# RMSNorm with ReLU on one core: the last store's last row divided between SyncE and GpSimd

## Chip, core and metric

One NeuronCore of a Trainium2 chip. The metric is the device time of one execution in microseconds (us), median of several. One profiled execution of each kernel gives the trace; its span, from the first to the last instruction, is about 1.8 us shorter than the device time of the same execution.

## The reference

```python
# x: 16 x 1024 x 512 float32, gamma: 512 ones, eps: 1e-5
rms = np.sqrt(np.mean(x ** 2, axis=-1, keepdims=True) + eps)
return np.maximum(x / rms * gamma, 0).astype(np.float32)
```

33.6 MB are read and 33.6 MB written; each row of 512 numbers is normalized by itself.

## The kernel before

The 16384 rows lie as 8 chunks of 128 partitions by K = 16 rows, so one partition's part of a chunk is 32 KB in one piece, in memory and in its slot. There are 6 slots. SyncE issues all large DMAs and waits in between; GpSimd only passes on semaphores; ScalarE makes sums of squares and square roots; VectorE the rest.

```python
    def store(i):
        nc.sync.dma_start(out=ov[i], in_=slot_ap(i)).then_inc(sem_slot[i % nslots], 16)

    with tc.tile_critical():
        # ... the first six chunks' loads
        for i in range(nchunks):
            nc.sync.wait_ge(done, per * (i + 1))
            store(i)
            # ... wait for a free slot and load the next chunk
        for m, (i, a, r) in enumerate(loads):
            loaded(nc.gpsimd, m)
            nc.gpsimd.sem_inc(ready, r // G)
        # ... ScalarE and VectorE loops; each half chunk ends with then_inc(done, 1)

    with nc.sync.register("landed") as landed:          # all stores have landed
        nc.sync.reg_mov(landed, 32)
        for s in range(nchunks - nslots, nslots):
            nc.sync.wait_ge(sem_slot[s], landed)
        nc.sync.reg_mov(landed, 64)
        for s in range(nchunks - nslots):
            nc.sync.wait_ge(sem_slot[s], landed)
```

At the end of the block `tile_critical` the framework has SyncE, ScalarE, VectorE and GpSimd each execute a DRAIN instruction (all four stand on that line in the traces), and SyncE waits for the others before it goes on to the waits named `landed`.

Of the kernel before, what the change touches and what calls it, by code (L numbers as in the profile page):

```python
# [12 lines left out]
@with_exitstack  # L13
def kernel(
    ctx: ExitStack,
    tc: tile.TileContext,
    x: bass.AP,
    gamma: bass.AP,
    eps: bass.AP,
    out: bass.AP,  # L20
):



    nc = tc.nc
    P = nc.NUM_PARTITIONS

    x2 = x.flatten_outer_dims()
    out2 = out.flatten_outer_dims()
    n, d = x2.shape  # L30
    rows = n // P
    inv_d = 1.0 / d
    K = 16
    G = 8
    nchunks = rows // K
    nslots = 6
    ngroups = rows // G
    per = K // G
    xv = x2.rearrange("(c p k) d -> c p k d", p=P, k=K)
    ov = out2.rearrange("(c p k) d -> c p k d", p=P, k=K)  # L40

    singles = ctx.enter_context(tc.tile_pool(name="singles", bufs=1))
    psum = ctx.enter_context(
        tc.tile_pool(name="psum", bufs=1, space=bass.MemoryType.PSUM))

    gseed = singles.tile([P, d], F32, name="gseed")
    gamma_sb = singles.tile([P, d], F32, name="gamma_sb")
    eps_sb = singles.tile([P, 1], F32, name="eps_sb")
    ss = singles.tile([P, rows], F32, name="ss")
    rms = singles.tile([P, rows], F32, name="rms")  # L50
    rstd = singles.tile([P, rows], F32, name="rstd")
    slots = singles.tile([P, nslots * K * d], F32, name="slots")
    junk = psum.tile([P, G, d], F32, name="junk")


    loads = [(0, 0, G), (0, G, K - G)] + [(i, 0, K) for i in range(1, nchunks)]


    sem_half = tc.alloc_semaphore("half")
    sem_slot = [tc.alloc_semaphore(f"slot{s}") for s in range(nslots)]  # L60
    sem_g = tc.alloc_semaphore("gam")
    sem_z = tc.alloc_semaphore("zero")
    ready = tc.alloc_semaphore("ready")
    sq = tc.alloc_semaphore("sq")
    done = tc.alloc_semaphore("done")
    sa = tc.alloc_semaphore("sa")
    sv = tc.alloc_semaphore("sv")

    def slot_ap(i):
        s = (i % nslots) * K * d  # L70
        return slots[:, s:s + K * d].rearrange("p (k d) -> p k d", d=d)

    def load(m):
        i, a, r = loads[m]
        nc.sync.dma_start(out=slot_ap(i)[:, a:a + r, :],
                          in_=xv[i][:, a:a + r, :]
                          ).then_inc(sem_half if m == 0 else sem_slot[i % nslots], 16)

    def loaded(engine, m):
        i = loads[m][0]  # L80
        if m == 0:
            engine.wait_ge(sem_half, 16)
        else:
            engine.wait_ge(sem_slot[i % nslots], 32 * (i // nslots) + 16)

    def store(i):
        nc.sync.dma_start(out=ov[i], in_=slot_ap(i)).then_inc(sem_slot[i % nslots], 16)

    ctx.enter_context(tc.manual_schedule(engines={mybir.EngineType.SP}))
    with tc.tile_critical():  # L90
        for m, (i, a, r) in enumerate(loads):
            if i < nslots:
                load(m)
        nxt = nslots
# [3 lines that stand above are left out]
            if i >= 1 and nxt < nchunks:  # L98
                nc.sync.wait_ge(sem_slot[nxt % nslots], 32)
                for m, (c, a, r) in enumerate(loads):  # L100
                    if c == nxt:
                        load(m)
                nxt += 1

        for m, (i, a, r) in enumerate(loads):
            loaded(nc.gpsimd, m)
            nc.gpsimd.sem_inc(ready, r // G)

        nc.vector.memset(gseed, 0.0).then_inc(sem_z, 1)  # L109
        nc.vector.memset(eps_sb, eps).then_inc(sem_z, 1)  # L110

        nc.scalar.wait_ge(sem_z, 1)
        nc.scalar.dma_start(out=gseed[0:P:32, :],
                            in_=gamma[None, :].to_broadcast([P // 32, d])
                            ).then_inc(sem_g, 16)
        nc.scalar.preload_act_table(ACTF.Sqrt)  # L116
        nc.scalar.wait_ge(sem_z, 2)
        with nc.scalar.Fori(0, ngroups) as gi:
            nc.scalar.wait_ge(ready, 1)
            nc.scalar.sem_inc(ready, -1)  # L120
            base = nc.scalar.snap((gi % (nslots * per)) * (G * d))
            col = nc.scalar.snap(gi * G)
            for j in range(G):
                a = nc.scalar.activation(  # L124
                    out=junk[:, j, :], in_=slots[:, bass.ds(base + j * d, d)],
                    func=ACTF.Square, accum_out=ss[:, bass.ds(col + j, 1)])
                if j == G - 1:
                    a.then_inc(sa, 1)
            nc.scalar.wait_ge(sa, 1)
            nc.scalar.sem_inc(sa, -1)  # L130
            nc.scalar.activation(out=rms[:, bass.ds(col, G)], in_=ss[:, bass.ds(col, G)],  # L131
                                 func=ACTF.Sqrt, bias=eps_sb, scale=inv_d).then_inc(sq, 1)

        nc.vector.wait_ge(sem_g, 16)
        nc.vector.stream_shuffle(gamma_sb, gseed, [0] * 32)  # L135
        with nc.vector.Fori(0, ngroups) as gi:
            nc.vector.wait_ge(sq, 1)
            nc.vector.sem_inc(sq, -1)  # L138
            base = nc.vector.snap((gi % (nslots * per)) * (G * d))
            col = nc.vector.snap(gi * G)  # L140
            blk = slots[:, bass.ds(base, G * d)]
            nc.vector.reciprocal(out=rstd[:, bass.ds(col, G)],  # L142
                                 in_=rms[:, bass.ds(col, G)]).then_inc(sv, 1)
            nc.vector.wait_ge(sv, 1)
            nc.vector.sem_inc(sv, -1)  # L145
            for j in range(G):
                row = slots[:, bass.ds(base + j * d, d)]
                r = nc.vector.scalar_tensor_tensor(  # L148
                    out=row, in0=row, scalar=rstd[:, bass.ds(col + j, 1)], in1=gamma_sb,
                    op0=ALU.mult, op1=ALU.mult)  # L150
                if j == G - 1:
                    r.then_inc(sv, 1)
            nc.vector.wait_ge(sv, 1)
            nc.vector.sem_inc(sv, -1)  # L154
            nc.vector.tensor_scalar_max(out=blk, in0=blk, scalar1=0.0).then_inc(done, 1)  # L155

    with nc.sync.register("landed") as landed:
        nc.sync.reg_mov(landed, 32)
        for s in range(nchunks - nslots, nslots):
            nc.sync.wait_ge(sem_slot[s], landed)  # L160
        nc.sync.reg_mov(landed, 64)
        for s in range(nchunks - nslots):
            nc.sync.wait_ge(sem_slot[s], landed)


# [33 lines left out]
```

## Time and profile before

| | before |
|---|---|
| device time, median of 6 | 162.75 us (162.68 to 163.0) |
| span | 160.9 us |
| DMA engines busy with SyncE's queue | 97.6% |
| last store issued | 146.46 us |
| last closing packet, its landing | 159.39 us, 159.88 us |
| SyncE's branch after its last wait | 159.95 us |

A store ends on each DMA engine with a packet of 4 B, the closing packet, and its increment of the semaphore lands some tenths of a us later (0.36 us for most engines and 0.49 for the last in this trace). The views that carry this stand in the prediction below and are not repeated. Of a line's instructions a view gives name, count, ns least/median/most, first and last start in us; on the line that ends the block (L90), SyncE's NOP is where it goes on when all others have drained.

```profile
L90 SPq NOP  x2: 13/13/13, 0.7 to 147.2; - x2
L90 POOLq DRAIN  x1: 41/41/41, 146.9 to 146.9; - x1
```

GpSimd's drain takes 41 ns, and at 147.2 us, 12.7 us before the last landing, SyncE is past the block. It then goes through its waits for the older slots while the last store is still running. When this lands, only the end of that wait and the branch are left before the closing barrier.

### The profile page before, as it was taken

Reading aid. Unit: us, or ns where it says so; the run is one execution under the profiler, and the core shown is the slowest. Engines: PE = TensorE matmul, PEld = TensorE weight load, DVE = VectorE, ACT = ScalarE, POOL = GpSimd, SP = SyncE. Lnnn points to the kernel's source line nnn. Section 1 sums busy time; section 2 is a strip of 40 time slices with the busy share of each in tenths; the row PEclk is TensorE's granted clock in tenths of the full one; section 3 lists DMA queues with packets and bytes.
Section 4 is the critical chain, followed back from the end, with each engine's and each line's share of the span. In section 5 each row is a group of like instructions: output and inputs, shape, how many; then the busy total and the mean of one; then the engine's idle time right before and its main releaser. Section 6 shows DMA issues by size and latency. Waiting matters only on the chain. (4 is left out here: it accounts for less than half of the span.)

```text
span 160.9 us, 1006 instructions
## 1 busy us (share of the span) xinstructions
DVE 126.0 (78%) x164; ACT 86.3 (54%) x273; POOL 0.2 (0%) x4
## 2 busy tenths in 40 slices
DVE  1103989898989899999999999999999999994000
ACT  3088929889988988988900198503994000000000
POOL 0000000000000000000000000000000000000000
DMA  5999999999999998999999999999999999999993
GB/s 155 434 432 415 521 391 391 513 399 391 489 424 391 481 432 367 415 391 489 424 391 489 424 391 448 464 391 440 456 407 432 456 415 424 464 415 424 464 407 138
DMA packets 2456, 67.12 MB, mean 417 GB/s; under 512 B 276, under 2 KB 276, under 8 KB 280
## 3 DMA queue, kind: packets, MB, share of 16 engines
q1 hardware_dynamic: 2448, 67.11, 97.6%
q10 hardware_dynamic: 8, 0.01, 0.0%
HBM read 33.56 MB, written 33.55 MB: 417 GB/s over the span
## 5 line engine op out<-in xcount | busy, mean ns | idle before, releaser
L124 ACT ACTIVATE junk<-slots 128x512 f32 x128 | 74.5, 582 | 30.6 <-ACTq L120 30.3
L148 DVE SCALAR_TENSOR_TENSOR slots<-slots,rstd,gamma_sb 128x512 f32 x128 | 86.2, 747 | 4.8 <-DVEq L145 4.8
L155 DVE TENSOR_SCALAR slots<-slots x16 | 36.7, 2294 | 2.4 <-DVEq L154 0.2
L124 ACT ACTIVATION_READ_ACCUMULATOR junk<-slots x128 | 23.9, 187 | 0.0
L142 DVE RECIPROCAL rstd<-rms x16 | 3.1, 196 | 6.3 <-DVEq L138 6.3
L131 ACT ACTIVATE rms<-ss,eps_sb x16 | 4.8, 301 | 3.0 <-ACTq L130 3.0
L135 DVE LOAD_MASK_SELECT gamma_sb<-gseed x1 | 0.0, 14 | 5.8 <-DMA gseed<-in_gamma_dram 5.8
L116 ACT ACT_TABLE_LOAD x1 | 1.3, 1283 | 2.8 <-issue 2.8
L109 DVE MEMSET gseed<- 128x512 f32 x1 | 0.5, 485 | 1.1 <-SPq L90 1.1
L135 DVE STREAM_SHUFFLE gamma_sb<-gseed 128x512 f32<-128x512 f32 x1 | 0.7, 715 | 0.0
L180 POOL MEMSET const-bfloat16-1.0<- 128x1 bf16 x1 | 0.1, 103 | 0.0
L180 POOL MEMSET const-uint8-127<- 128x1 uint8 x1 | 0.1, 102 | 0.0
L180 POOL MEMSET const-float32-0.0<- 128x1 f32 x1 | 0.1, 100 | 0.2 <-issue 0.2
L180 POOL MEMSET const-float32-1.0<- 128x1 f32 x1 | 0.1, 99 | 0.0
L110 DVE MEMSET eps_sb<- 128x1 f32 x1 | 0.1, 59 | 0.0
## 6 DMA issues: line engine op xcount, KB each, us to landing
out_dram<-slots SPq DMA_DIRECT2D x8, 4096.0 KB, 31.3
slots<-in_x_dram SPq DMA_DIRECT2D x7, 4096.0 KB, 30.3
slots<-in_x_dram SPq DMA_DIRECT2D x2, 2048.0 KB, 9.6
gseed<-in_gamma_dram ACTq DMA_DIRECT2D x1, 8.0 KB
```

The source lines that it names most:

```text
L109: nc.vector.memset(gseed, 0.0).then_inc(sem_z, 1)
L110: nc.vector.memset(eps_sb, eps).then_inc(sem_z, 1)
L116: nc.scalar.preload_act_table(ACTF.Sqrt)
L124: a = nc.scalar.activation(out=junk[:, j, :], in_=slots[:, bass.ds(base + j * d, d)], func=ACTF.Square, accum_out=ss[:, bass.ds(col + j, 1)])
L131: nc.scalar.activation(out=rms[:, bass.ds(col, G)], in_=ss[:, bass.ds(col, G)], func=ACTF.Sqrt, bias=eps_sb, scale=inv_d).then_inc(sq, 1)
L135: nc.vector.stream_shuffle(gamma_sb, gseed, [0] * 32)
L142: nc.vector.reciprocal(out=rstd[:, bass.ds(col, G)], in_=rms[:, bass.ds(col, G)]).then_inc(sv, 1)
L148: r = nc.vector.scalar_tensor_tensor(out=row, in0=row, scalar=rstd[:, bass.ds(col + j, 1)], in1=gamma_sb, op0=ALU.mult, op1=ALU.mult)
L155: nc.vector.tensor_scalar_max(out=blk, in0=blk, scalar1=0.0).then_inc(done, 1)
L180: nc = _bacc.Bacc("TRN2", target_bir_lowering=False, num_devices=1)
```

## The change

The packet records of the trace show one DMA engine ending the last store alone, 0.37 us after the next. The change is to give the engine thought to be it (the fifth, number 4) less to do: the last row of the last store goes to other engines, by way of GpSimd's DMAs.

```diff
+    parts = [(0, P, 0, K)]
+    tail = [(0, P, 0, K - 1), (125, P, K - 1, K)]
+    tail_pool = [(0, 5, K - 1, K), (5, 125, K - 1, K)]
+
+    def store_part(engine, i, part, sem):
+        p0, p1, k0, k1 = part
+        engine.dma_start(out=ov[i][p0:p1, k0:k1, :], in_=slot_ap(i)[p0:p1, k0:k1, :]
+                         ).then_inc(sem, 16)
+
     def store(i):
-        nc.sync.dma_start(out=ov[i], in_=slot_ap(i)).then_inc(sem_slot[i % nslots], 16)
+        for part in (tail if i == nchunks - 1 else parts):
+            store_part(nc.sync, i, part, sem_slot[i % nslots])
@@ in the block, after GpSimd's loop
+        nc.gpsimd.wait_ge(done, ngroups)
+        for part in tail_pool:
+            store_part(nc.gpsimd, nchunks - 1, part, sem_tail)
@@ at the end
-        nc.sync.reg_mov(landed, 64)
+        nc.sync.wait_ge(sem_tail, landed)
         for s in range(nchunks - nslots):
+            last = tail if s == nchunks - nslots - 1 else parts
+            nc.sync.reg_mov(landed, 48 + 16 * len(last))
             nc.sync.wait_ge(sem_slot[s], landed)
```

## The prediction

> **What bounds the kernel now.** I read the page first, then the SyncE queue's waits, then the DMA view in ever narrower windows around the end. The page of the kernel before:
>
> ```profile
> span 160.9 us, 1006 instructions
> DVE 126.0 (78%) x164; ACT 86.3 (54%) x273; POOL 0.2 (0%) x4
> DMA  5999999999999998999999999999999999999993
> DMA packets 2456, 67.12 MB, mean 417 GB/s; under 512 B 276, under 2 KB 276, under 8 KB 280
> q1 hardware_dynamic: 2448, 67.11, 97.6%
> ```
>
> The DMA engines are full in 38 of 40 slices, while the busiest compute engine, DVE, has 22% idle. All of it is one queue, q1, that SyncE issues: nine loads and eight stores. So the kernel is bound by 67.1 MB through 16 DMA engines, and compute ends early: the last DVE instruction runs from 144.14 for 2.29 us (timeline), and the last store is issued at 146.46. What SyncE's own queue waits for from there on, and the line where it waits:
>
> ```profile
> SPq L87 <- DVE slots L155: 16.1, 1, 16.1
> SPq L163 <- DMA out_dram<-slots: 12.4, 1, 12.4
> ...
> DMA to landing us min/median/max: 13.4/31.3/41.0
> ```
>
> The last 12.4 us are a wait for a store. The least time to landing, 13.4 us, is the last store's: 146.46 + 13.4 = 159.9 us. The span ends 1.0 us later, after the closing barrier. A store of 4096 KB is 128 packets of 32 KB, 8 for each of 16 engines, and one packet of 4 B for each engine that announces its end. The DMA view from 149.72 to 158.3, inside the last store:
>
> ```profile
> DMA packets 112, 3.67 MB, mean 428 GB/s; under 512 B 0, under 2 KB 0, under 8 KB 0
> q1 hardware_dynamic: 112, 3.67, 99.0%
> ```
>
> 0.990 x 16 x 8.58 us / 112 = 1.213 us for 32 KB. The view from 5.7 to 6.4 us, where the small gamma load runs on q10, gives the price of a 2 KB packet:
>
> ```profile
> q10 hardware_dynamic: 4, 0.01, 3.0%
> ```
>
> 0.030 x 16 x 0.7 / 4 = 0.084 us. A straight line through both is 0.009 us a packet plus 0.0376 us a KB; it gives 0.611 us for 16 KB, which is what the packet records of the first two half loads show. So a 30 KB packet should take 1.138 us.
>
> Which engine ends last? The closing 4 B packets in 158.3 to 158.9, in 158.95 to 159.1, and in 159.1 to 159.45:
>
> ```profile
> DMA packets 13, 0.00 MB, mean 0 GB/s; under 512 B 13, under 2 KB 13, under 8 KB 13
> ...
> DMA packets 2, 0.00 MB, mean 0 GB/s; under 512 B 2, under 2 KB 2, under 8 KB 2
> ...
> DMA packets 1, 0.00 MB, mean 0 GB/s; under 512 B 1, under 2 KB 1, under 8 KB 1
> ```
>
> 13 of 16 engines are done by 158.9 (the records say 158.37 to 158.82), two at 159.01 and 159.03, and a single one at 159.40. Their announcements land about 0.36 us after the packet for the others, and 0.49 us for the last (159.37 and 159.88). The records of the earlier stores show one engine falling behind: the last closing packet trails the next by 0.02 us near 110.6, then by 0.09 near 120.4, 0.19 near 130.2, 0.29 near 140.0, 0.37 near 149.7 and 0.37 at 159.4. So the end of the kernel is one DMA engine's lag, some 0.4 to 0.5 us. That is what this change aims at.
>
> [...] The trace before has no GpSimd DMA and no engine numbers: it neither confirms the numbering nor says that the late engine is number 4. [...]
>
> **The change part by part.** Bytes are the same. Removed: the last store's row 15 from all packets, so SyncE's main piece has 128 packets of 30 KB, 8 an engine: 8 x 1.138 = 9.10 us instead of 8 x 1.213 = 9.70. Moved: row 15 as 128 packets of 2 KB: 5 and 120 by GpSimd, 3 (partitions 125 to 127) by SyncE[...]. Per engine, if the dealing is as intended:
> - number 4: 9.10 + 1 x 0.084 = 9.19 us, 0.52 less than now;
> [...]
>
> If the late engine is number 4, it ends at 159.40 - 0.52 = 158.88 and lands at about 159.37. The next two, at 159.01 and 159.03 now, become last[...]; plus 0.36 to land, 159.46 to 159.63. Against 159.88 this saves 0.42 to 0.25 us, 0.35 in the middle. Costs: GpSimd's two issues[...] begin at 146.46 and lie beside 12 us of transfers; SyncE's second issue (0.33 us, as its issues show) as well; extra closing packets, 0.01 us each. The wait on the tail's semaphore comes before those on slots 0 and 1, and two more register moves: under 0.1 us, and only if GpSimd's part lands last. [...] I put these costs at 0.07 us in all. Sum: -0.35 + 0.07 = about -0.28 us, so 162.72 - 0.28 = 162.44.
>
> **The rivals.**
> First, the skipped engine is not the late one[...]. Then the late engine gets 0.07 to 0.24 us more, and the time is 162.8 to 163.0. Against it: an edit this particular was surely made by someone who knew the late engine; for it: nothing in the trace says which engine it is. I give it 25%.
> Second, a new wait takes the place: [...] its small packets[...] drain after the main piece. With 12 us of room I expect little, [...] 163 us or more: 10%.
> Third, using GpSimd for DMA at all adds something at start or end ([...] a longer drain in the closing barrier). Nothing in the profile speaks for it: GpSimd's drains take 34 to 88 ns now. If it did, 163 to 165 us: 5%.
> Fourth, the lag is random from execution to execution. Against it: three runs within 0.32 us, and the same engine falling behind over several stores. Then the gain would fade to about 0.1.
>
> **Range and chances.** The largest possible gain is perfect balance: the mean engine ends near 158.7, so 0.7 us, 0.4%. A 2% change is 3.25 us and would need a fixed cost that nothing shows. Intended course 162.25 to 162.55; rivals up to about 163; so 162.44, range 162.15 to 163.0, and 1%, 98%, 1%.
>
> **What would show it.** Right: a new GpSimd queue with 125 packets of 2 KB and its closing packets, 128 packets of 30 KB at 1.138 us in q1, closing packets of the main piece within 158.4 to 159.3 and none at 159.4, the last landing near 159.5 instead of 159.88, the span near 160.6. Wrong: one engine still alone at 159.4 or later (first rival); GpSimd's 2 KB packets after the 30 KB ones (second); the distance from the last landing to the end of the span over 1.0 us, or the unprofiled time further than 1.8 us from the span (third).

The sum is -0.35 + 0.07 = -0.28 us, so 162.44. The saving of 0.42 to 0.25 us was made with assumed shares: one 2 KB piece for number 4, as stands above, and 8 to 10 for each of the other engines, which was to make the next two 0.07 to 0.24 us later (159.10 to 159.27). The 0.07 us of costs held 0 to 0.1 us for the small packets' turns. The cut guess at the length of GpSimd's issues is not in the sum; in the result's trace they took 0.63 and 0.55 us. The shares were never shown; what the traces show instead is told under the experiments.

## The result

The changed kernel took 163.5 us (163.3 to 163.74, 6 runs) against 162.75 (162.68 to 163.0, 6 runs). The ratio is 1.0044, interval 1.0031 to 1.0057. So it is 0.75 us slower by the medians, within 2%, but outside the predicted range, and on the other side of the time before than the 162.44 predicted.

The page of the changed kernel:

```profile
span 161.8 us, 1009 instructions
DVE 126.0 (78%) x164; ACT 86.3 (53%) x273; POOL 1.4 (1%) x6
...
DMA packets 2575, 67.12 MB, mean 415 GB/s; under 512 B 327, under 2 KB 327, under 8 KB 399
...
q1 hardware_dynamic: 2454, 66.85, 96.6%
q0 software_dynamic: 112, 0.26, 0.4%
```

Compute and bytes are the same. GpSimd's queue q0 has 112 packets, not the predicted 125 of 2 KB and their closing packets: the records show 5 of 2 KB, 60 of 4 KB (two 2 KB pieces each, 0.159 us), 43 of 4 B and 4 of 8 B. What SyncE's own queue waits for has changed its form:

```profile
SPq L97 <- DVE slots L173: 105.0, 6, 26.5
SPq L76 <- DMA out_dram<-slots: 33.2, 2, 24.2
SPq L105 <- POOLq L105: 12.8, 1, 12.8
```

The 12.4 us for a DMA have become 12.8 us for GpSimd, at L105, the end of the block. The instructions of that line:

```profile
L105 SPq NOP  x2: 13/13/13, 0.7 to 160.4; - x2
...
L105 POOLq DRAIN  x1: 13069/13069/13069, 147.3 to 147.3; - x1
```

GpSimd's drain took 41 ns before and takes 13.07 us now, to 160.41 us. The last of GpSimd's DMAs landed at 160.28. SyncE goes on at 160.44 and only then begins the waits for slots that had been done for long. The profile names no cause for these 13 us. As the drain's record, from 147.34 to 160.41 us, ends 0.13 us after that landing, they are read as the drain lasting until then; run 8 below tests it. SyncE's branch behind all waits, before and after:

```profile
L194 SPq COMPARE_BRANCH  x2: 33/33/33, 0.8 to 159.9; - x2
```

```profile
L214 SPq COMPARE_BRANCH  x2: 33/33/33, 0.8 to 160.8; - x2
```

And the end of the last store after, the closing packets in 159.0 to 159.3, 159.3 to 159.75 and 159.75 to 159.9 us:

```profile
DMA packets 4, 0.00 MB, mean 0 GB/s; under 512 B 4, under 2 KB 4, under 8 KB 4
...
DMA packets 0, 0.00 MB, mean 0 GB/s; under 512 B 0, under 2 KB 0, under 8 KB 0
...
DMA packets 2, 0.00 MB, mean 0 GB/s; under 512 B 2, under 2 KB 2, under 8 KB 2
...
q0 software_dynamic: 1, 0.00, 0.4%
q1 hardware_dynamic: 1, 0.00, 0.4%
```

One engine is still alone at the end, now by 0.63 us, and it has a closing packet of GpSimd's queue as well as one of SyncE's. From the trace's records, in us, for the engine that ends last:

| step | before | after | more |
|---|---|---|---|
| it closes the store before the last | 149.71 | 149.99 | 0.29 |
| from there to its last closing packet | 9.68 | 9.81 | 0.13 |
| from that packet to its landing | 0.49 | 0.67 | 0.18 |
| from the landing to SyncE's branch | 0.07 | 0.37 | 0.30 |
| from the branch to the end of the span | 0.95 | 0.96 | 0.01 |

(The column of differences is taken before rounding.) The sum is 0.91, as much as the spans differ. The first row lies before any packet of the change has run. The eleven profiled executions of the experiments below, with and without the change, have 149.73 to 150.18 at that point, so it is read as chance of the execution; it may be so in part only. The three rows in the middle, 0.61 us together, lie within the timed interval (0.0031 to 0.0057 of 162.75 is 0.50 to 0.93 us).

### The profile page after: what moved, and what is told of

It reads as the page before. It is cut to its first block, busy times and chain, and to the rows that moved or that the text cites. A ratio compares the mean times of both kernels' runs of the same rounds, so it can differ in the third digit from the quotient of the medians. Undisturbed runs are those within 1.5% of the kernel's fastest.

```text
span 161.8 us, 1009 instructions
## 1 busy us (share of the span) xinstructions
DVE 126.0 (78%) x164; ACT 86.3 (53%) x273; POOL 1.4 (1%) x6
## 5 line engine op out<-in xcount | busy, mean ns | idle before, releaser
L97 POOL DMA_DIRECT2D out_dram<-slots x2 | 1.2, 588 | 146.3 <-DVE slots L173 146.3
```

The source lines that it names most:

```text
L97: engine.dma_start(out=ov[i][p0:p1, k0:k1, :], in_=slot_ap(i)[p0:p1, k0:k1, :]).then_inc(sem, 16)
```

## The experiments

The theory (the drain theory): GpSimd's drain at the block's end lasts until its DMAs have landed, so SyncE's closing waits, hidden before, come one after the other behind the last landing. Beside it stand two questions: which engine is the late one, and which does GpSimd's second DMA leave out? The rivals: a fixed cost of GpSimd's DMAs wherever they are issued, and a cost of smaller packets. Eleven kernels ran on three chips; all results were correct. Runs 1, 2, 8 and 11 are single runs, so their state is unknown; of these only run 8's time is used.

### 1 and 2: marking the engines

```diff
+        for j in range(2, 16):          # in SyncE's queue, behind the last store
+            c0 = 2 * j * (j - 1) - 4
+            nc.sync.dma_start(out=gseed[0:j, c0:c0 + 4 * j],
+                              in_=x2[0:j, 0:4 * j]).then_inc(sem_mark, 16)
```

and a wait for `sem_mark` at the end. In one run this was added to the kernel before:

> The kernel before with fourteen tiny marker loads queued by SyncE behind the last store: the j-th goes to j partitions with rows of 16 j bytes, j from 2 to 15, [...] the rows that follow the last store on an engine tell its number (15 minus the number of markers, for engines 1 to 15). The time is of no interest, it grows by the markers. Theory A (the change skips the right engine in principle, something else ate the gain): the engine that closes the last store last, 0.3 to 0.5 us behind the next, has number 4 and shows 11 markers. Theory B (the late engine isn't the fifth): it shows another number of markers.

In the other, to the changed kernel:

> The same markers in the changed kernel. It tells two things at once: the number of the late engine, and the number of the engine that GpSimd's second DMA leaves out (the one whose chain shows only packets of 8 B in GpSimd's queue). Theory A: both are number 4 (11 markers). Theory B: the engine left out is number 4 (11 markers) and the late one, closing about 0.4 to 0.6 us after the next, another, with the four 4 KB packets of GpSimd in its chain.

The traces hold no engine numbers. A number here is a label read from the markers: j - 1 for an engine whose first marker is the one of j partitions (packets of 16 j bytes in these two runs). The label tells nothing of the hardware's own names.

The times (165.38 and 165.25 us, one run each) are those of the markers and tell nothing else. In the kernel before, the late engine's last 32 KB packet ended at 159.98 us, and from there on it alone carried markers of 80, 96, 112, and so on to 240 B, which are j = 5 to 15: eleven, so number 4. A second engine was late in this execution, closing at 159.68, with markers for 14 and 15 only: number 13. In the changed kernel the late engine (closing at 159.65) again showed 80 B as its first marker: number 4. So far theory A was right.

The engine left out was another matter. It closed first, at 158.04 us, after four packets of 8 B in GpSimd's queue. Following packets of known length from closing to closing gives one sequence for it, without a 2 KB packet of GpSimd's first DMA, while the late engine has one of those and four pairs of 4 KB. No marker followed the left-out engine's closing where markers for low numbers were waiting. So it was not number 4. With this the rest of theory A fell, and theory B too: the change had not lightened the late engine. That it was number 15, the label left for an engine that shows none of these markers, was a conjecture here; run 11 tests it.

### 3: the same division by SyncE alone

```diff
-    tail = [(0, P, 0, K - 1), (125, P, K - 1, K)]
-    tail_pool = [(0, 5, K - 1, K), (5, 125, K - 1, K)]
+    tail = [(0, P, 0, K - 1), (0, P, K - 1, K)]       # and nothing on GpSimd
```

> No GpSimd: SyncE issues the last store as 15 rows and then the last row of all 128 partitions, so every engine has the same bytes as before in eight more packets (8 x 0.009 us). Drain theory (the loss comes from GpSimd's drain at the end of the block, which holds back SyncE's closing waits until the GpSimd DMAs have landed): no GpSimd DMA, no drain, so 162.75 + 0.1, at most 162.9 us. Splitting theory (smaller packets and a second closing packet cost it): 163.2 to 163.5 us.

Measured: 162.73 us, ratio to before 1.0000 (0.9987 to 1.0014). Smaller packets cost nothing that can be seen, and that part of the splitting theory falls. Its second closing packet is not tested here: SyncE's two closing packets on the late engine are 0.65 us apart, with the eight small packets between them, where the changed kernel's are back to back. The branch came 0.02 us after the last landing.

### 4: GpSimd's part from the store before the last

```diff
-        for part in (tail if i == nchunks - 1 else parts):
+        for part in (tail if i == nchunks - 2 else parts):
-        nc.gpsimd.wait_ge(done, ngroups)
+        nc.gpsimd.wait_ge(done, ngroups - per)
-            store_part(nc.gpsimd, nchunks - 1, part, sem_tail)
+            store_part(nc.gpsimd, nchunks - 2, part, sem_tail)
```

> The same division into SyncE and GpSimd DMAs, but of the store before the last, so that GpSimd's DMAs land near 150 us and its drain ends some 9 us before the end. Drain theory: SyncE's closing waits are again over by then but for the last, the last landing is followed by the branch within 0.07 us instead of 0.38, and the time is 162.7 to 162.9 us. Rival (using GpSimd for DMA has a fixed cost at start or end, whenever it is issued): 163.3 to 163.5 us.

Measured: 162.82 us, ratio 1.0011 (0.9997 to 1.0024). The wait list of SyncE's queue and the block's end:

```profile
SPq L214 <- DMA out_dram<-slots: 9.6, 1, 9.6
```

```profile
L105 SPq NOP  x2: 13/13/13, 0.7 to 147.2; - x2
...
L105 POOLq DRAIN  x1: 223/223/223, 146.9 to 146.9; - x1
```

The drain, at 0.22 us, is short again, SyncE passes the block at 147.2 us as before, its last wait is once more for a DMA, and the branch came 0.02 us after the last landing. The GpSimd DMAs had landed at 142.62, earlier than expected. A fixed cost of using GpSimd for DMA, of the size of the loss, is ruled out.

### 5: the changed kernel again

> The changed kernel again, for a comparison on one chip with the next two and for a second profile. Drain theory: 163.3 to 163.6 us; GpSimd's drain ends 0.1 us after its last DMA landed, SyncE then needs 0.4 us for seven instructions, the branch comes 0.3 to 0.4 us after the last landing; the engine that GpSimd leaves out is again one that had no 2 KB packet of GpSimd's first DMA, and the late one did have one and has all four pairs.

Measured: 163.39 us, ratio 1.0036 (1.0018 to 1.0054), on another chip. The four steps of the table were there again: 9.81 us for the last store on the late engine, 0.67 to land, 0.37 from landing to branch, and 149.89 for the first row. The late engine again had one 2 KB packet and four pairs. For the left-out engine the records are again consistent with none of the first DMA.

### 6: only the five partitions on GpSimd

```diff
-    tail = [(0, P, 0, K - 1), (125, P, K - 1, K)]
-    tail_pool = [(0, 5, K - 1, K), (5, 125, K - 1, K)]
+    tail = [(0, P, 0, K - 1), (5, 125, K - 1, K), (125, P, K - 1, K)]
+    tail_pool = [(0, 5, K - 1, K)]
```

> GpSimd moves only the 5 partitions; SyncE issues the 120 itself [...]. Drain theory: the drain ends near 154.4 us, SyncE's closing waits are over in time, and no second closing packet follows the last on the late engine: 162.65 to 162.95 us. Rival (the loss is in the packets and in which engine carries them): 163.3 to 163.6 us as the changed kernel.

Measured on the chip of run 5: 162.91 us, ratio 1.0009 (0.9991 to 1.0026).

```profile
L105 SPq NOP  x2: 13/13/13, 0.7 to 154.1; - x2
...
L105 POOLq DRAIN  x1: 5672/5672/5672, 148.4 to 148.4; - x1
```

The drain ends at 154.03 us; GpSimd's DMA had landed at 153.95. The drain follows its DMA, and ended in time it cost nothing that can be seen. That each engine carries the same bytes in runs 5 and 6 was assumed. The medians of runs 5 and 6 differ by 163.39 - 162.91 = 0.48 us, and the two steps of the table that run 6 is without, 0.18 and 0.30, sum to 0.48. (In the two traces the stretch from the closing of the store before the last to the branch differs by 0.52 us.) The step of 0.18 can be seen by itself: in run 6 the late engine ended with one closing packet, which landed after 0.47 us; in runs 3 and 4 it was 0.48 each. In the result, in run 5 and in run 7 there were two closing packets back to back on that engine, and the second landed after 0.67 us in all three, 0.19 us after the first.

### 7: fewer waits behind the drain

```diff
+        for s in range(nchunks - nslots, nslots):     # still inside the block
+            nc.sync.wait_ge(sem_slot[s], 32)
+        nc.sync.wait_ge(sem_slot[0], 64)
@@ at the end: only sem_tail and the last slot are still waited for
```

> The changed kernel, with SyncE's waits for the five slots that are long done put ahead of the block's end, so that after GpSimd's drain only the waits for its tail and for the last slot remain: three instructions fewer of 0.066 us each. Drain theory: 0.2 us less than the changed kernel in the same rounds, about 163.25 us, with the branch about 0.2 us after the last landing. If the drain isn't on the path, no change.

Measured: 163.18 us, ratio 1.0026 (1.0008 to 1.0044), 0.21 us under run 5 of the same rounds. The intervals of the two overlap; the trace:

```profile
L215 SPq COMPARE_BRANCH  x2: 33/33/33, 0.8 to 160.5; - x2
```

The branch came 0.18 us after the last landing (160.32) instead of 0.37. The instructions behind the drain are on the path here, about 0.066 us each (in the result's trace the last four of them begin at 160.58, 160.65, 160.71 and 160.78 us and the branch at 160.85).

### 8: a late DMA that nobody waits for

```diff
+        nc.gpsimd.wait_ge(sem_slot[(nchunks - 1) % nslots], 64)
+        nc.gpsimd.dma_start(out=gseed[0:1, 0:128], in_=x2[0:1, 0:128]).then_inc(sem_late, 16)
```

> The kernel before, with one load of 512 bytes by GpSimd into a dead buffer, issued once the last store has landed; no instruction waits for its semaphore. Drain theory: the drain at the end of the block holds everybody until it has landed, so 2 to 5 us more, 165 to 168 us, and SyncE's closing waits after it. If a DMA holds the end only through an explicit wait: 162.7 to 163.3 us (GpSimd's issue alone).

Measured: 165.13 us, one run; its span was 163.4. (The 2 to 5 us of the expectation were a guess, made from no trace.)

```profile
SPq L91 <- POOLq L91: 14.8, 1, 14.8
```

```profile
L91 SPq NOP  x2: 13/13/13, 0.7 to 162.0; - x2
...
L91 POOLq DRAIN  x1: 1817/1817/1817, 160.2 to 160.2; - x1
```

The last store had landed at 159.91 us, GpSimd's load at 161.92; the drain ended at 162.00. No wait on a semaphore asks for this load, and the kernel ends 2.4 us later than before. That is the drain theory's effect without the rest of the change.

### 9 and 10: six more packets for engines 0 to 3, or 0 to 4

```diff
+        for q in range(6):              # behind the last store; 5 for 4 in the other run
+            p0 = 4 * q
+            nc.sync.dma_start(out=gseed[p0:p0 + 4, :], in_=x2[p0:p0 + 4, :]
+                              ).then_inc(sem_dose, 16)
```

> The kernel before with six loads of 4 partitions by 2 KB into a dead buffer queued by SyncE behind the last store: 0.56 us more for engines 0 to 3 and none for the others. Theory that the end is engine number 4's: engines 0 to 3, which close around 158.7 us, close near 159.3 and the end hardly moves: 162.7 to 162.95 us (one more wait, 0.06 us). Rival (the late engine in the timed runs is among 0 to 3, or every transfer at the end costs): about 163.3 us.

> The same with 5 partitions, so that engine number 4 has the six packets too. Theory: the end moves by 0.5 to 0.7 us against the kernel with 4 partitions, to 163.2 to 163.6 us. Rival (the late engine has a number over 4, or differs from run to run): no difference between the two.

Measured: 163.17 us with four partitions (ratio 1.0025, 0.9982 to 1.0068) and 164.05 with five (1.0066, 1.0026 to 1.0107). The difference of 0.88 has the direction of the theory, but both missed their ranges: the loads landed 1.0 to 1.1 us after their closing packets, where the stores take 0.4 to 0.5, so that with four partitions too it was a load that ended the kernel (160.25 us, the store 159.97). The records show why: with five partitions the late engine closes its six loads 0.086 us apart, but they land 0.19 us apart (160.21, 160.40, 160.59, 160.78, 160.96, 161.15). The expectation priced the packets and not this queue of landings. As a measure of time the pair is not clean. The intervals are wide because one run each of the kernel before (164.65 us) and of the one with four partitions (164.41 us) took 1.9 and 1.2 us more than its median. The records are clean. The DMA view from 159.35 us to 160.1 with four partitions, then from 159.45 with five:

```profile
DMA packets 1, 0.00 MB, mean 0 GB/s; under 512 B 1, under 2 KB 1, under 8 KB 1
```

```profile
DMA packets 13, 0.01 MB, mean 19 GB/s; under 512 B 7, under 2 KB 7, under 8 KB 13
```

With four, the late engine closes its store and is done; with five, its closing packet is followed by six packets of 2 KB and their closings. So it has the fifth share: number 4, on a further chip.

### 11: another place to divide, with markers

```diff
-    tail = [(0, P, 0, K - 1), (125, P, K - 1, K)]
-    tail_pool = [(0, 5, K - 1, K), (5, 125, K - 1, K)]
+    tail = [(0, P, 0, K - 1)]
+    tail_pool = [(0, 8, K - 1, K), (8, P, K - 1, K)]
@@ markers of 4, 5, 8, 15 and 16 partitions behind the last store
```

> The changed kernel with GpSimd's division at 8 partitions instead of 5 (8, then 120; SyncE's three partitions fall away) and five marker loads of 4, 5, 8, 15 and 16 partitions behind the last store. [...] the second DMA leaves out number 7, which had a 2 KB packet of the first and shows three markers (8, 15, 16). [...] it leaves out number 15, which had none of the first and shows one marker (16 partitions); the late engine shows four markers (5, 8, 15, 16).

The text sets two outcomes against each other: the gap moves with the division, to number 7, or it is at number 15.

Measured: 163.93 us, one run. Records of two engines (start in us, bytes, queue; SyncE's 30 KB packets, the 4 B packets of GpSimd's first DMA and of the markers, and what the late engine did earlier are left out):

```
left out:  153.862 8 q0, 155.002 8 q0, 156.142 8 q0, 157.282 8 q0, 158.439 4 q0, 158.445 4 q1, 158.451 512 q1
late:      159.693 4 q0, 159.699 4 q1, 159.705 160 q1, 159.722 256 q1, 159.742 480 q1, 159.770 512 q1
```

The late engine shows the markers for 5, 8, 15 and 16 partitions: number 4. The left-out one shows the marker for 16 alone, which by the labels makes it number 15, and no packet of the first DMA. Moving the division from 5 to 8 did not move the gap. GpSimd's copy of 120 partitions is 60 packets of 4 KB in the result's trace, four to an engine where they were followed; with number 15 left out, that is engines 0 to 14, eight partitions each. The late engine's packet of 2 KB fits a first copy to engines from 0 up, one partition each.

## Why the prediction was wrong

**Right:** the bound (SyncE's queue and one late engine), its number 4 (three runs with markers and the pair of runs 9 and 10), the prices of packets (30 KB 1.138 us, 2 KB 0.084), the turn-taking of the queues packet by packet (in the result's trace the 8 B packets of GpSimd's queue on the left-out engine begin at 154.96, 156.10, 157.24 and 158.38 us, 1.14 us apart, the time of one 30 KB packet), and GpSimd's data being through with the main piece: its last data packet on the late engine ended before the last 30 KB one. (One small misreading: 37 of the 40 slices of the page before are at 90% or more, and one is at 80 to 90%.)

**The step on dealing failed.** The prediction gave number 4 one small packet and 9.19 us. It had nine 2 KB pieces, one of GpSimd's first DMA and eight of the second in four pairs: 8 x 1.138 + 0.084 + 4 x 0.159 = 9.82 us, against 9.81 measured. The gain of 0.42 to 0.25 us that the sum starts from is therefore missing, and 0.13 us was lost instead. This was the first rival, the skipped engine not being the late one, to which 25% were given; its 0.07 to 0.24 us for the late engine, an estimate from assumed shares at the measured prices, holds the 0.13. The sum was made for a dealing that no trace had shown. The rival's 162.8 to 163.0 us was too little, because the next step was missing from it also.

**The step on costs failed.** "Under 0.1 us, and only if GpSimd's part lands last", 0.07 us in all, was 0.48 us. The sum counted the wait on the tail's semaphore and took the older waits for hidden, as they had been. It overlooked that the block's closing drain stands between GpSimd's DMAs and those waits: 0.30 us, shown by runs 4, 6, 7 and 8. It also priced a second closing packet at 0.01 us, where back to back on the late engine it delayed the last landing by 0.18 us (three profiles with, four without). That one engine's landings come about 0.19 us apart was seen with other DMAs too, in run 10 and at the ends of the runs with markers. The third rival had "a longer drain in the closing barrier" at 5%, with the remark that drains take 34 to 88 ns now; those were drains with no GpSimd DMA in flight, which tell nothing of one that has. The drain that grew was the one at the block's end; the closing barrier took 0.95 us before and 0.96 us after. That the time lies within the third rival's 163 to 165 us, and within the second's "163 us or more", is therefore in part luck: the third had the wrong drain, and of the second's late small packets nothing was seen.

**The sum, mended:** 0.13 + 0.18 + 0.30 = 0.61 us, against medians 0.75 and 0.67 us apart in the two comparisons. What remains is within the intervals.

**Open:** what leaving out the right engine would have brought, since both divisions tried, at 5 and at 8 partitions, gave number 4 a share and left another engine out; why number 4 falls behind in the stretch of stores; whether the 0.29 us of the first row are all chance; and why one engine's landings come 0.19 us apart. No version beat the kernel before: the best of those tried (runs 3, 4 and 6) are level with it.

## What to carry to other kernels

In these kernels a DMA that GpSimd issued late inside the block held up what came after the block, even where no semaphore asked for it (run 8, 2.4 us). So issue it early (run 4, ratio 1.0011 to the kernel before), or put all finished waits ahead of the block's end (run 7, 0.21 us). Before shifting bytes between DMA engines, mark the engines with tiny DMAs of known partition counts and see where the shares really go. Closing packets count too: where several came close together on the last engine, each landed 0.19 us after the one before. A wait that was hidden is hidden only as long as nothing new comes to stand before it (here 0.30 us came of that): in a sum of costs, ask of each new instruction what its engine must reach before it can go on.

## Measured besides

- GpSimd's copy of 120 partitions left one engine out in every profile whose records were followed, whether 5 or 8 partitions had gone before. In the result's trace it is 60 packets of 4 KB (two 2 KB pieces each, so eight partitions for each of fifteen engines), and engines without a share have packets of 4 or 8 B in GpSimd's queue (11 and 4 of them).
- GpSimd's drain took 13.07 us in the result against 0.041 in the kernel before, which has no GpSimd DMA, and ended 0.08 to 0.13 us after the landing of GpSimd's DMAs in seven profiles.
- Of two closing packets back to back on one engine the second landed after 0.67 us; one alone landed after 0.47 to 0.49. In run 10 seven landings of one engine came 0.19 to 0.20 us apart.
- On the idle engines of run 8 the first packet of GpSimd's DMA ran 0.68 us after the issue had ended, 1.28 us after it began. In the result, on engines busy with another queue, the first packet of GpSimd's queue ran at 151.61 us, 4.3 us after the first issue had ended (147.33).
- The late engine was number 4, with and without GpSimd DMAs in flight, in all five runs that tell the engines apart. Its last large packet ended 0.28 to 0.85 us after the next engine's, which in one of them was number 13's.
- SyncE's issues got longer where several small DMAs followed each other on few engines behind a large one: 1.00 to 1.04 us for the third to the sixth in runs 9 and 10, against 0.33 for the store. What those issues waited for was not examined.
